# Direct products by halves of time in place of seven half-size products: gated unit and output projection

## The chip, the cores and the metric

The kernel runs on one core of a Trainium2 chip. The metric is the device time in microseconds (us) of one execution. Engines: PE is TensorE (matmul), DVE is VectorE, ACT is ScalarE, POOL is GpSimd, SP issues most DMAs.

## The reference, cut to what matters

A trunk of two layers on a stream of 1024 tokens by 1024 features. Layer 0 mixes by a long convolution beside a differential attention, joined by one output projection `w_out`; layer 1 mixes by a gated unit; each is followed by a convolutional feed-forward block (FFN).

```python
# layer 0, first mixer (y_a: convolution, y_b: attention, 512 features each)
return jnp.concatenate([y_a, y_b], axis=-1) @ w_out
# layer 1, gated unit
u, v = jnp.split(jax.nn.gelu(h @ w_in + b_in, approximate=False), 2, axis=-1)
v = layernorm(v, ln_g, ln_b)
vb = v.reshape(B, n, CHUNK, SGU_GROUPS, D_SGU // SGU_GROUPS)
s = jnp.einsum('gts,bnsgc->bntgc', w_s, vb) + b_s.T[:, :, None]
return (u * s.reshape(B, L, D_SGU)) @ w_out
# in both layers
x = x + g1 * mix_x
x = x + g2 * conv_ffn(modulate(rmsnorm(x, norm_ffn_g[i]), sh2, sc2), *ffn)
```

Four matrix products of 1024 x 1024 x 1024 are concerned: `w_out` of layer 0, the two halves (u and v) of the gated unit's `w_in`, and its `w_out`.

## The kernel before, in words

**Tiles.** The stream lies as eight tiles of 128 features x 1024 times; `H0` and `H1` are the two halves of 512 times. Every operand of a large product is split in two (`hilo`, L1149 to L1154): ACT rounds it to the upper part (the cast, L1152), DVE or POOL subtracts it from the operand for the lower part (through the helper at L128), and `mm3` issues three matmuls of 128 x 512 (L149): upper by upper, upper by lower, lower by upper. A 1024 x 1024 x 1024 product taken directly is 128 such groups, 384 matmuls.

**Seven half-size products.** Before, each such product is made of seven of half size, M1 to M7 (48 matmuls each, 336 in all). They take sums of the weight's quarters (`wsums`) and of the operand's quarters (`in_place`, or the blocks B11, B21 and T1 to T4 that `norm` writes), and each result is added to one or more quarters of the output (`gated_sum`, `accum`). `down_steps` cuts M1 to M7 into steps of one k (12 matmuls).

**The planner.** `run` goes through a list of `Step`s. Before a step's matmuls (`use`) it issues the loads of steps up to `ahead` further on, and the splits (`prep`) of steps up to `prep_ahead` further on. `Later` holds generators that put a few instructions of other work (norms, the unit's centring) between steps. The letters of tables such as `E_W` say for each split whether DVE (V) or POOL (G) subtracts. Each engine does its instructions in program order; so does each DMA queue.

**First mixer.** `heads` runs the attention. In its last heads, products M1, M2 and M6 of the output projection (`product`, 144 matmuls) fill PE between the scores, in the PSUM banks of the scores. `out_proj` does M7, M4, M5 and M3 (192 matmuls) after the attention, adds them to the stream, squares it for the row norm, and starts the FFN's norm.

**Gated unit.** `sgu` first forms u by Winograd products (`up_phase`), adds bias and Gelu and writes it to memory (`ud`); then v (`down_steps(2, ...)`), its bias, Gelu and centring by layer norm (`center`); mixing by positions in 128 x 128 matmuls; then u is read back, multiplied, and the output product follows (`down_steps(3, ...)`). Layer 0's FFN (FFN0) comes before it, layer 1's (FFN1) behind it.

```python
def hilo(x, elo=None, new=unit):
    t = new(F32R)
    A.copy(out=t[:, H0], in_=x)
    sub(elo or G, t[:, H1], x, t[:, H0])
```

Of the kernel before, what the change touches and what calls it, by code (L numbers as in the profile page):

```python
# [11 lines left out]
F32 = mybir.dt.float32  # L12
# [47 lines left out]
E_U, E_V, E_B, E_C = ("VVVV",) * 3, ("VVVV",) * 5, ("GGGGGGGG",), ("GGGGVVVV",) * 2  # L60
PO = "wtap"
# [27 lines left out]
def tile_kernel(ctx: ExitStack, tc: tile.TileContext, ap: dict, out: bass.AP, stop=None):  # L89
# [703 lines left out]
    def attention(fp, x):  # L793

        with ExitStack() as es:
# [132 lines left out]
            wb, spare, aux = {}, [], None  # L928

            def two_rows(src, k, n=2):  # L930

                r = spare.pop(0) if spare else W.pool.tile([P, 2, 512], F32, tag="wraw", name=nm("wraw"))
                ld(r[:, :n], src[k : k + n].rearrange("k p n -> p k n"))
                return r

            def parts(name, tag):
                if tag == "p":
                    t = [pp.tile([P, NKEY], F32R, tag="p", name=nm("p"), bufs=PB) for _ in range(4)]
                    hi, lo = ([t[2 * i + k // 2][:, HALF[k % 2]] for k in range(4)] for i in range(2))
                else:  # L940
                    hi, lo = ([t[:, k * 512 : (k + 1) * 512] for k in range(4)] for t in (f8(F32R), f8(F32R)))
                wb[name] = hi, lo
                return hi, lo

            def operand(name, src):

                hi, lo = parts(name, "f8")
                raw = []
                for k in (0, 2):
                    raw.append(raw_unit(src[k : k + 2].rearrange("k p n -> p k n")))  # L950
                    yield
                for k in range(4):
                    x = raw[k // 2][:, HALF[k % 2]]
                    A.copy(out=hi[k], in_=x)
                    sub(V if k == 3 else G, lo[k], x, hi[k])
                    yield

            def operand3(name, a, b, c, op, tag, last=None):

                hi, lo = parts(name, tag)  # L960
                for k in (0, 2):
                    x, y, z = two_rows(a, k, 2 if k == 0 or last is None else 1), two_rows(b, k), two_rows(c, k)
                    yield
                    for i in range(2):
                        xi = x[:, i] if k + i < 3 or last is None else last
                        yi = y[:, i]
                        op(V, yi, xi, yi)
                        (sub if op is add else add)(V, yi, yi, z[:, i])
                        A.copy(out=hi[k + i], in_=yi)
                        sub(G, lo[k + i], yi, hi[k + i])  # L970
                        yield
# [7 lines left out]
            def operands():  # L979
                yield from operand("w1", ap["wabo"][0:4][:, :, H0])  # L980
                yield from operand("w2", ap["wabo"][4:8][:, :, H0])
                yield from operand("b1", yd[0:4][:, :, H0])
                wo = ap["wabo"]
                yield from operand3("w6", wo[0:4][:, :, H1], wo[4:8][:, :, H1], wo[0:4][:, :, H0], add, "p")

            def product(m):

                (wh, wl), (bh, bl) = wb["w" + m[1]], wb["b" + m[1]]
                accum = gated_sum(x, mods[0][:, 16:24])
                ps = [scores_bank(j // 2)[:, :1024] if j % 2 == 0 else None for j in range(4)]  # L990
                ps = [ps[j // 2 * 2][:, HALF[j % 2]] for j in range(4)]
                order = [(k, j) for j in range(4) for k in range(4)] if m != "M6" else [(k, j) for k in range(4) for j in range(4)]
                for n, (k, j) in enumerate(order):
                    js = slice(j * P, (j + 1) * P)
                    mm3(ps[j], wh[k][:, js], wl[k][:, js], bh[k], bl[k], k == 0, k == 3)
                    if k == 3:
                        accum(m, j, ps[j])
                    if n % 4 == 3:
                        yield
# [4 lines left out]
            def heads():  # L1004
                nonlocal aux
                aux = f8(F32).rearrange("p (a n) -> p a n", a=4)
                V.memset(aux[:, 0, 0:1], 0.0)
# [19 lines left out]
                def nrm():  # L1027
                    if norms and next(norms[0], 1):
                        norms.pop(0)

# [54 lines left out]
                for _ in side:  # L1085
                    pass
                for _ in product("M1"):
                    pv()
                    nrm()
                for _ in operand("b2", yd[4:8][:, :, H0]):  # L1090
                    pass
                for _ in range(2):
                    r = f8(F32).rearrange("p (a k n) -> p a k n", a=2, k=2)
                    spare.extend((r[:, 0], r[:, 1]))
                b6 = operand3("b6", yd[4:8][:, :, H1], yd[0:4][:, :, H1], yd[0:4][:, :, H0], sub, "p", aux[:, 3])
                for _ in product("M2"):
                    pv()
                    nrm()
                    nrm()
                    next(b6, None)  # L1100
# [3 lines left out]
                for _ in b6:  # L1104
                    pass
                for _ in product("M6"):
                    pass
# [90 lines left out]
    class Stream:  # L1198
        T = None

# [33 lines left out]
    def norm(x, sqs, l, a, b):  # L1234
# [39 lines left out]
        for n, i in (("T1", 0), ("B22", 4)):  # L1274
            for k in range(4):

                T[n][k] = hilo(x[i + k][:, H1], E(E_5[s], i + k), unit if i + k == 0 else xunit)
                yield k % 2

# [173 lines left out]
    def residual(s, x, gate, dst, after):  # L1453
# [17 lines left out]

        def done(m):
# [8 lines left out]
    def then_norm(x, a, b):  # L1481
        return lambda l, sqs: Later.add(norm(x, sqs, l, a(), b()), N0[sqs.s][l])

# [3 lines left out]
    def out_proj(x):  # L1487
        y, ts = [None] * NK, [None] * 4
        def bload(m, k):
            if m == "M7":  # L1490
                for i in (k, k + 4):
                    y[i] = unit()
                    ld(y[i], yd[i])

        def bprep(m, k, _):
            return hilo(in_place(0, m, k, y[k], y[k + 4], ts, "M7"), E(E_O[0], k))

        acc, done, start = residual(0, x, mods[0][:, 16:24], xs[0], then_norm(x, lambda: A2[0], lambda: mods[0][:, 24:32]))
        start()
        if T3P:  # L1500
            t = unit()
            G.memset(t[:, 0:1], 0.0)
            ts[0:2] = [t[:, H0], t[:, H1]]
        steps = down_steps(0, 4, ap["wabo"], bload, bprep, acc, done, products=ORDER[3:])
        for s in steps[4:]:
            s.ahead = 16
        prep = steps[SQ].prep
        steps[SQ].prep = lambda: (prep(), done("M2"))
        return steps
# [80 lines left out]
    def sgu(x_src, dst):  # L1590
        ud = dram.tile([NK, P, S], F32, name="ud")
        v, u, t3, k_ = [None] * NK, [None] * NK, [None] * 4, {}

        def post(m, c1, c2):
            for c, g in ((c1, m), (c2, m + 4)):
                A.activation(c, c, AF.Gelu, bias=col("sbu", g))
                st(ud[g], c)
# [19 lines left out]
        def accum(m, j, p):  # L1617
            if m == "M1":
                for t in (j, j + 4):
                    v[t] = unit()  # L1620
                    A.copy(out=v[t].rearrange("p (a n) -> p a n", a=2), in_=p[:, None, :].to_broadcast([P, 2, 512]))
                return
            for i, l in {"M2": [(0, 0)], "M6": [(None, 1), (1, 0)], "M7": [(1, 0), (1, 1)], "M4": [(1, 0)],
                         "M5": [(None, 1)], "M3": [(0, 1)]}[m]:
                y = v[j + 4 * l]
                if i is None:
                    y, p_ = y.rearrange("p (a n) -> p a n", a=2), p[:, None, :].to_broadcast([P, 2, 512])
                else:
                    y, p_ = y[:, HALF[i]], p
                add(V, y, y, p_)  # L1630

        def bias():
            for t in range(NK):
                add(E(E_B[0], t), v[t], v[t], k_["bv"])
                yield 1

        def center(l):


            for t in range(4 * l, 4 * l + 4):  # L1640
                x = v[t]
                A.activation(x, x, AF.Gelu)
# [10 lines left out]
            yield MIXWAIT  # L1653
            for k in range(4):
                for g in (k, k + 4):
                    ps, t = bank(), unit()[:, H0]
                    for n in range(4):
# [153 lines left out]
```

## Time and profile before

| quantity | us |
|---|---|
| median of three runs (2870.97 to 2883.97) | 2875.83 |
| the profiled execution | 2883.27 |
| its span on the core | 2881.5 |
| output projection and first norm, 933 to 1050 | 117 |
| FFN0, 1090 to 1793 | 703 |
| gated unit, 1793 to 2122 | 329 |
| FFN1 and final norm, 2190 to the end | 691.5 |

Times within a stage are read in us from the span's start. A view by windows tells how long each engine was busy in a stretch and which clock PE was granted (1.00 is full speed). The timeline lists an engine's instructions, and in brackets the idle time ahead of them and what ended it. A matmul "b<-u,u" reads two split operands and writes a PSUM bank.

### The profile page before, as it was taken

How to read it: one execution, taken by the hardware profiler on the slowest of the kernel's cores; microseconds unless marked ns; L12 is line 12 of the kernel's file. 1: busy time of each engine (PE TensorE's matmuls, PEld its weight loads, DVE VectorE, ACT ScalarE, POOL GpSimd, SP SyncE). 2: the span in 40 equal slices, each digit the busy share in tenths (PEclk: the TensorE clock that was granted, in tenths of full speed). 3: DMA queues.
4: the chain of work that ended last, by engine and by line, in shares of the span. 5: the costliest groups of instructions: out<-in, count | busy, mean ns of one | idle time of the engine just before them, and what ended most of it. 6: DMA issues, size and time to landing. Idle time of an engine off the chain costs nothing. (4 is left out here: it accounts for less than half of the span.)

```text
span 2881.5 us, 30329 instructions
## 1 busy us (share of the span) xinstructions
PE 2496.0 (87%) x11000; PEld 1965.2 (68%) x11000; DVE 2267.2 (79%) x2425; ACT 1072.5 (37%) x1561; POOL 1610.4 (56%) x986
## 2 busy tenths in 40 slices
PE   6899668777988679999999898899769999999897
PEld 2797556565766456777777686677557777777676
DVE  4676887866998788988887967868978888886954
ACT  2322111115664244334334344532344343344242
POOL 1323665544443664655556777545765555657785
PEclk9899888888999889999999999899879999999999
DMA  7133221256741532454456533243112323227422
GB/s 269 63 135 125 73 88 44 83 181 199 212 121 63 204 110 85 162 174 154 143 168 244 174 127 99 60 163 107 49 54 68 112 75 102 93 72 274 139 84 103
DMA packets 137574, 363.97 MB, mean 126 GB/s; under 512 B 12587, under 2 KB 25391, under 8 KB 135248
## 3 DMA queue, kind: packets, MB, share of 16 engines
q1 hardware_dynamic: 90768, 259.25, 28.0%
q10 hardware_dynamic: 46656, 102.78, 9.5%
q8 instruction: 87, 1.43, 0.2%
q14 instruction: 63, 0.52, 0.1%
HBM read 271.80 MB, written 90.18 MB: 126 GB/s over the span
## 5 line engine op out<-in xcount | busy, mean ns | idle before, releaser
L149 PE MATMUL b<-u,u 128*128 128x512 f32 x5780 | 1417.3, 403 | 151.4 <-POOL u L128 96.7
L149 PEld LDWEIGHTS b<-u,u 128*128 128x128 f32 x5780 | 1106.7, 195 | 459.3 <-POOL u L128 133.1
L128 POOL TENSOR_TENSOR u<-u,u 128x512 fp32r<-128x512 f32 (+2 forms) x641 | 1030.7, 1631 | 586.8 <-ACT u L1152 456.6
L128 DVE TENSOR_TENSOR u<-u,u 128x512 fp32r<-128x512 f32 (+2 forms) x569 | 640.9, 1155 | 209.6 <-ACT u L1152 133.4
L1152 ACT CAST u<-u 128x512 fp32r<-128x512 f32 x772 | 438.1, 616 | 600.1 <-DVE u L128 419.3
L124 DVE SCALAR_TENSOR_TENSOR u<-u,cols,u 128x1023 f32<-128x1023 f32 x176 | 303.8, 1729 | 23.8 <-ACT u L1520 23.0
L128 DVE TENSOR_TENSOR u<-u,b 128x512 f32<-128x512 f32 (+1 forms) x368 | 248.4, 690 | 28.5 <-PE b L149 22.8
L149 PE MATMUL b<-x,u 128*128 128x512 f32 x1008 | 246.2, 398 | 0.0
L128 POOL TENSOR_TENSOR f<-f 128x256 f32<-128x256 f32 (+2 forms) x99 | 124.7, 1273 | 210.9 <-DVE f L128 181.4
L149 PEld LDWEIGHTS b<-x,u 128*128 128x128 f32 x1008 | 190.4, 189 | 49.3 <-issue 4.2
L128 DVE TENSOR_TENSOR f<-f 128x256 f32<-128x256 f32 (+3 forms) x178 | 178.5, 1052 | 1.1
L124 DVE SCALAR_TENSOR_TENSOR x<-b,mods,x 128x512 f32<-128x512 f32 (+1 forms) x140 | 124.7, 938 | 37.8 <-PE b L149 37.8
L149 PE MATMUL pj<-hh,whi 128*128 128x512 f32 x320 | 131.5, 411 | 24.2 <-DVE t L124 14.0
L1520 ACT ACTIVATE u<-u,cols 128x1024 f32<-128x1024 f32 x88 | 109.3, 1244 | 94.4 <-DVE u L128 93.8
L128 POOL TENSOR_TENSOR p<-p,p 128x1280 f32<-128x1280 f32 x27 | 79.4, 2942 | 99.2 <-ACT p L880 78.7
L149 PE MATMUL pj<-hh,wlo 128*128 128x512 f32 x320 | 129.8, 406 | 2.4 <-DVE wlo L128 1.6
L149 PE MATMUL pj<-hl,whi 128*128 128x512 f32 x320 | 130.6, 408 | 0.0
L1532 ACT ACTIVATE u<-u 128x1024 f32<-128x1024 f32 x44 | 46.7, 1061 | 162.3 <-DVE u L124 162.2
L128 POOL TENSOR_TENSOR wlo<-wraw,whi 128x1024 fp32r<-128x1024 f32 x24 | 63.2, 2635 | 75.5 <-ACT whi L143 64.3
L869 ACT ACTIVATE p<-s,nx 128x1280 f32<-128x1280 f32 x64 | 85.0, 1329 | 43.9 <-DVE nx L865 39.9
L149 PE MATMUL s<-f,f 128*128 128x512 f32 (+1 forms) x288 | 86.2, 432 | 17.3 <-ACT t L768 9.9
L865 DVE TENSOR_REDUCE nx<-s 128x1 f32<-128x1280 f32 x64 | 94.5, 1479 | 3.8 <-PE s L149 3.3
(222 smaller groups left out, 2936.2 us busy)
## 6 DMA issues: line engine op xcount, KB each, us to landing
u<-wup SPq DMA_DIRECT2D x88, 512.0 KB, 3.6
Td<-u ACTq DMA_DIRECT2D x66, 512.0 KB, 3.8
u<-Td SPq DMA_DIRECT2D x56, 512.0 KB, 5.0
wraw<-modw SPq DMA_DIRECT2D x48, 512.0 KB, 4.4
u<-wdown SPq DMA_DIRECT2D x40, 512.0 KB, 6.5
wraw<-modw0b SPq DMA_DIRECT2D x32, 512.0 KB, 3.9
xs<-x ACTq DMA_DIRECT2D x48, 256.0 KB, 2.5
x<-xs SPq DMA_DIRECT2D x24, 512.0 KB, 4.3
```

The source lines that it names most:

```text
L124: eng.scalar_tensor_tensor(out=o, in0=a, scalar=sc, in1=b, op0=op0, op1=op1)
L128: eng.tensor_tensor(out=o, in0=a, in1=b, op=op)
L149: T.matmul(o, l, r, start=st, stop=sp)
L865: V.reduce_max(out=q.nx, in_=q.s, axis=AX.X, negate=True)
L869: A.activation(q.p[m], q.s, AF.Exp, bias=q.nx, accum_out=q.l[:, m : m + 1])
L1152: A.copy(out=t[:, H0], in_=x)
L1520: A.activation(a, c, AF.Identity, bias=col(f"fb{l}", f), scale=col(f"fw{l}1", f))
L1532: A.activation(g, g, AF.Silu)
```

## The change

All four products are taken directly, by halves of time: `l` is the half of time, `c` the half of the output's features, `k` the 128 input features of a step.

- In the attention's last heads, `mixed` splits the eight operand tiles of the first half of time and `columns` the weights (from `wabm`, the same weight laid out by blocks of output features); `product` does the whole first half of time, eight groups of 24 matmuls, in the score banks. Operand tile 7 waits for the last head norm of that half (`norms_done`).
- `out_proj` becomes 16 steps of `direct_steps` for the second half of time. Squares of the first half start at its first split.
- The norm in front of the gated unit becomes `norm_direct`: eight splits per half, no sums.
- The gated unit forms v first, with bias and Gelu at its eviction, centres each half of time (`center`), mixes, then forms u (16 steps of 24 matmuls), multiplies it at once (`gate`) and goes on to the output product. u is no longer written to memory.
- In the instruction streams PE has 10356 matmuls instead of 10164 (48 more in the first mixer, 144 more in the gated unit); DVE has 2191 instructions instead of 2419, ACT 1655 instead of 1727, POOL 922 instead of 991.

```diff
+SV, SW, SO, SP = (8, 3), (4, 2), (8, 4), (16, 4)
+E_H, E_X, E_Y = ("VGVGVGVG", "VGVGVGVG"), "VGVG", ("VGVGVGVG", "VGVGVGVG")
+A_Y, A_W = "GGGVGGVV", "GGVGVGVG"
...
+            def product():
+
+                for m in range(NK):
+                    if m % 2 == 0:
+                        ps = scores_bank(m // 2 % 2)
+                    while m not in wb:
+                        yield True
+                    p = ps[:, HALF[m % 2]]
+                    for k in range(NK):
+                        while yb[k] is None:
+                            yield True
+                        kk = slice(k * P, (k + 1) * P)
+                        mm3(p, wb[m][0][:, kk], wb[m][1][:, kk], *yb[k], k == 0, k == NK - 1)
...
+                    y = x[m][:, H0]
+                    stt(V, y, p, gate[:, m : m + 1], y, MUL, ADD)
...
+    def norm_direct(x, sqs, l, a, b):
...
+        for k in range(NK):
+            mul(E(E_M[s], k), x[k][:, c], x[k][:, c], R)
+            A.activation(x[k][:, c], x[k][:, c], AF.Identity, bias=b[:, k : k + 1], scale=a[:, k : k + 1])
+            Stream.H[l][k] = hilo(x[k][:, c], E(E_H[l], k), xunit if l and k else unit)
...
+        def prep(l, c, k):
+            if l == ls[0]:
+                w[c, k] = hilo(raw.pop((c, k)), E(E_X, k % 4))
+            if c == 0 and bsrc is not None:
+                bs[l, k] = hilo(bs[l, k], E(E_X, (k + 1) % 4))
+
+        def use(l, c, k):
...
+            for j in range(4):
+                js = slice(j * P, (j + 1) * P)
+                if swap:
+                    mm3(ps[j], bh[:, js], bl[:, js], wh, wl, k == 0, k == NK - 1)
+                else:
+                    mm3(ps[j], wh[:, js], wl[:, js], bh, bl, k == 0, k == NK - 1)
...
     def out_proj(x):
...
-        steps = down_steps(0, 4, ap["wabo"], bload, bprep, acc, done, products=ORDER[3:])
...
+        steps = direct_steps(ap["wabo"], None, acc, done, *SP, ls=(1,), bsrc=yd)
+        prep = steps[0].prep
+        steps[0].prep = lambda: (prep(), done(0, 0), done(0, 1))
...
+        def accum(l, c, j, p):
+            t = 4 * l + j
+            if c == 0:
+                v[t] = unit()
+            add(V, v[t][:, HALF[c]], p, k_["bv"][:, HALF[c]])
+            A.activation(v[t][:, HALF[c]], v[t][:, HALF[c]], AF.Gelu)
...
+            t = mixed[g][:, HALF[l]]
+            mul(E(E_C[l], g), t, t, u)
+            y[l][g] = hilo(t, E(E_Y[l], g))
...
-        steps = up_phase([(m, ap["wsu"][m], ap["wsu"][m + 4]) for m in range(4)], post, 1)
-        vs = down_steps(2, 4, ap["wsv"], None, None, accum, done, resident=True)
...
+        steps = direct_steps(ap["wsv"], lambda l, k: Stream.H[l][k], accum, done, *SV, swap=True)
...
-        steps += down_steps(3, 4, ap["wso"], lambda m, k: None, bprep, acc, dn, (x, x_src))
+        steps += direct_steps(ap["wso"], lambda l, k: y[l][k], acc, dn, *SO, x=(x, x_src))
```

SP, where the second half's loads of the output projection begin (`yd` is the mixed stream in memory, `wabo` the weight). Before:

```order
L933 DMA wraw_5870<-yd 128x2x512 [waits Pool_49]
L933 DMA wraw_5872<-yd 128x2x512 [waits DMAHW0_49,Pool_49]
L1357 DMA u_5979<-wabo 128x2x512 [waits DMAHW4_49,DMAHW0_49,DVE_49]
L1357 DMA u_5981<-wabo 128x2x512 [waits DMAHW5_49]
L1357 DMA u_5983<-wabo 128x2x512 [waits DMAHW6_49]
```

and of the changed kernel:

```order
L181 DMA wraw_5814<-wabm 128x1024 [waits DMAHW1_49,DVE_49]
L1510 DMA u_5979<-yd 128x2x512 [waits DMAHW7_49,DVE_49,PE_49]
L1514 DMA u_5981<-wabo 128x2x512 [waits DMAHW2_49,DMAHW1_49,Pool_49]
L1510 DMA u_5983<-yd 128x2x512 [waits DMAHW2_49]
L1514 DMA u_5985<-wabo 128x2x512 [waits DMAHW3_49]
```

The first of these loads takes a tile whose memory the score product's operands hold, so that it now waits for PE too.

POOL in the same stage, around the first half's row norm (`sv` is its variance, `x_...<-x_...,u_6106` its products with the broadcast row, `u_5993` raw weights). Before:

```order
L1502 MEMSET u_5974 128x1
L128 TENSOR_TENSOR u_6000<-u_5979,u_6000 128x512
L128 TENSOR_TENSOR u_6006<-u_5974,u_6006 128x512
L128 TENSOR_TENSOR u_5974<-u_5993,u_5991 128x512
L128 TENSOR_TENSOR u_5991<-u_5991 128x512
L128 TENSOR_TENSOR u_5991<-u_5993,u_5991 128x512
```

and of the changed kernel:

```order
L1212 TENSOR_TENSOR sv_6103<-sv_6103,mhalf 128x4
L132 TENSOR_TENSOR u_6114<-u_5991,u_6114 128x512
L132 TENSOR_TENSOR x_5103<-x_5103,u_6106 128x512
L132 TENSOR_TENSOR x_5111<-x_5111,u_6106 128x512
L132 TENSOR_TENSOR x_5107<-x_5107,u_6106 128x512
L132 TENSOR_TENSOR u_6139<-x_5109,u_6139 128x512
L132 TENSOR_TENSOR u_6142<-u_5993,u_6142 128x512
```

The sums of operands and weights are gone; the last row, the lower part of the weight of step k = 7, now stands behind three products of the norm.

PE in the gated unit, where the second half of time is mixed (128x128, `u_123..` are centred tiles of v). Before:

```order
L149 MATMUL b_13328<-u_13246,u_13243 128x512
L149 MATMUL b_13343<-u_12505,u_12656 128x128
L149 MATMUL b_13351<-u_12505,u_12656 128x128
L149 MATMUL b_13379<-u_12505,u_12656 128x128
L149 MATMUL b_13387<-u_12505,u_12656 128x128
L149 MATMUL b_13328<-u_13246,u_13243 128x512 x2
```

and of the changed kernel:

```order
L153 MATMUL b_12373<-u_12128,x_11990 128x512 x3
L153 MATMUL b_12545<-u_11722,u_12351 128x128
L153 MATMUL b_12551<-u_11722,u_12351 128x128
L153 MATMUL b_12565<-u_11481,u_12471 128x512 x3
L153 MATMUL b_12565<-u_11504,u_12471 128x512 x3
L153 MATMUL b_12545<-u_11722,u_12354 128x128
```

The mixing moved from the middle of the output product to a place directly behind the last product of v.

## Rows read from the trace of the kernel before

**Rows 1.** The page's busy time: us, share of the span, instructions.

```profile
PE 2496.0 (87%) x11000; PEld 1965.2 (68%) x11000; DVE 2267.2 (79%) x2425; ACT 1072.5 (37%) x1561; POOL 1610.4 (56%) x986
```

**Rows 2.** Windows: length, busy of PE, PEld, DVE, ACT, POOL; PE's clock; DMA.

```profile
1090.00:1793.00 703.00, 680.90 (x3029) 529.77 (x3029) 581.35 (x574) 292.59 (x444) 430.23 (x267) 0.98 0.46 155
1793.00:2122.00 329.00, 280.24 (x1164) 218.72 (x1162) 267.64 (x327) 128.28 (x203) 189.65 (x126) 0.91 0.28 95
2190.00:2881.50 691.50, 628.60 (x2614) 495.27 (x2612) 526.93 (x501) 262.68 (x391) 441.02 (x289) 0.97 0.34 115
...
966.40:1049.50 83.10, 56.40 (x210) 41.73 (x210) 72.28 (x79) 32.39 (x57) 66.45 (x37) 0.79 0.39 138
```

**Rows 3.** Timeline of PE, output projection: start, length, count, idle before and releaser.

```profile
941.81 1.10 PE L149 MATMUL tr<-f,ones 128*128 128x512 f32 x2 [0.39 <-DVE f L242]
...
965.41 0.96 PE L149 MATMUL s<-p,p 128*128 128x512 f32 x3 [0.88 <-DVE x L124]
973.37 0.79 PE L149 MATMUL b<-u,u 128*128 128x512 f32 x1 [7.00 <-ACT u L1152]
983.33 5.09 PE L149 MATMUL b<-u,u 128*128 128x512 f32 x12 [9.17 <-POOL u L128]
...
994.03 18.44 PE L149 MATMUL b<-u,u 128*128 128x512 f32 x71 [1.81 <-POOL u L128]
```

**Rows 4.** Timeline of PE in the gated unit.

```profile
1797.23 1.05 PE L149 MATMUL b<-ones,u 128*128 128x1 f32 x8 [1.26 <-DVE u L128]
...
1818.12 4.64 PE L149 MATMUL b<-u,u 128*128 128x512 f32 x10 [2.31 <-POOL u L128]
...
1890.06 22.88 PE L149 MATMUL b<-u,u 128*128 128x512 f32 x99
...
1974.00 1.95 PE L149 MATMUL b<-u,u 128*128 128x128 f32 x16
...
2034.42 0.80 PE L149 MATMUL b<-u,u 128*128 128x512 f32 x1 [5.00 <-ACT u L1152]
...
2130.77 1.87 PE L149 MATMUL b<-ones,u 128*128 128x1 f32 x8 [5.45 <-DVE u L128]
```

**Rows 5.** Timeline of DVE: a head norm, last evictions of three stages, the centring.

```profile
933.04 0.73 DVE L124 SCALAR_TENSOR_TENSOR f<-f,sg,tr 128x512 f32<-128x512 f32 x1
...
1047.54 2.79 DVE L124 SCALAR_TENSOR_TENSOR x<-b,mods,x 128x512 f32<-128x512 f32 x4
...
1791.25 2.79 DVE L124 SCALAR_TENSOR_TENSOR x<-b,mods,x 128x512 f32<-128x512 f32 x4 [4.38 <-PE b L149]
...
1987.80 0.68 DVE L1645 BATCH_NORM_STATS2 st<-u 128x6 f32<-128x512 f32 x1
...
1998.05 0.81 DVE L1651 TENSOR_SCALAR u<-u,mv,rs 128x1024 f32<-128x1024 f32 x1 [0.66 <-POOL rs L1650]
...
2119.77 2.73 DVE L124 SCALAR_TENSOR_TENSOR x<-b,mods,x 128x512 f32<-128x512 f32 x4 [1.96 <-PE b L149]
```

**Rows 6.** Groups of the gated unit, 1793 to 2122: count, busy us, mean ns.

```profile
L128 POOL TENSOR_TENSOR u<-u,u 128x512 fp32r<-128x512 f32 x69 | 105.3, 1545 | 53.4 <-ACT u L1152 48.3 <-DVE u L128 5.0
L1152 ACT CAST u<-u 128x512 fp32r<-128x512 f32 x115 | 64.8, 617 | 121.0 <-DVE u L128 81.2 <-POOL u L128 27.1 <-PE b L149 7.4
...
L128 DVE TENSOR_TENSOR u<-u,u 128x512 fp32r<-128x512 f32 x44 | 53.6, 1232 | 20.0 <-ACT u L1152 20.0
L128 DVE TENSOR_TENSOR u<-u,b 128x512 f32<-128x512 f32 x52 | 33.8, 677 | 14.6 <-PE b L149 12.6 <-DMA u<-wsv 2.0
```

**Rows 7.** Timeline of POOL: one subtraction with DVE quiet beside it.

```profile
941.96 1.28 POOL L128 TENSOR_TENSOR f<-wraw,f 128x512 fp32r<-128x512 f32 x1 [1.41 <-ACT f L954]
```

**Rows 8.** SP's queue: start, time that four issues took.

```profile
953.07 1.91 SPq L1357 DMA_DIRECT2D u<-wabo  x4
```

**Rows 9.** DMA issues: count, KB each, median us from issue to landing.

```profile
u<-yd SPq DMA_DIRECT2D x8, 512.0 KB, 8.7
...
f<-yd SPq DMA_DIRECT2D x3, 512.0 KB, 3.6
```

More of the change, by code (lines that the diff above doesn't have):

```diff
@@ L951, in operand @@
                     yield
[L952 to L955, printed above, removed]
-                    yield
[L958 to L962, printed above, removed]
-                    yield
[L964 to L971, printed above, removed]
+                for k, r in enumerate(raw + [aux[:, 2]] * (4 - len(raw))):
+                    while k0 + k == 7 and norms_done[0] < 7:
+                        yield
+                    A.copy(out=hi[k], in_=r)
+                    sub(E(A_Y, k0 + k), lo[k], r, hi[k])
+                    yb[k0 + k] = hi[k], lo[k]
+                    yield
@@ L979, in operands @@
             def operands():
[L980 to L999, printed above, removed]
+                yield from mixed(0)
+                for m in range(2):
+                    yield from columns(m)
+                yield from mixed(4)
+            def product():
[10 more added lines that the diff above has]
+                        mm3(p, wb[m][0][:, kk], wb[m][1][:, kk], *yb[k], k == 0, k == NK - 1)
+                        if k == 3:
+                            yield
+                    y = x[m][:, H0]
+                    stt(V, y, p, gate[:, m : m + 1], y, MUL, ADD)
+                    yield
             class Obj:
@@ L1499, in out_proj @@
[L1499 to L1503, printed above, removed]
-        steps = down_steps(0, 4, ap["wabo"], bload, bprep, acc, done, products=ORDER[3:])
[L1505 to L1508, printed above, removed]
+        acc, done, _ = residual(0, x, mods[0][:, 16:24], xs[0],
+                                then_norm(x, lambda: A2[0], lambda: mods[0][:, 24:32]), True)
@@ L1590, in sgu @@
     def sgu(x_src, dst):
[L1591 to L1597, printed above, removed]
+        v, mixed, y, k_ = [None] * NK, [None] * NK, [[None] * NK, [None] * NK], {}
         def consts():
@@ new lines, in sgu, with done, gate, uload @@
+        mixed_n = [0, 0]
+        def done(l, c):
+            if (l, c) == (0, 0):
+                Later.add(offsets())
+            if c:
+                Later.add(center(l))
+        def gate(g, l, u):
+            while mixed_n[l] <= g:
+                yield 1
+            t = mixed[g][:, HALF[l]]
+            mul(E(E_C[l], g), t, t, u)
+            y[l][g] = hilo(t, E(E_Y[l], g))
+        w = {}
+        def uload(m):
+            w[m] = unit()
+            ld(w[m], ap["wsu"][m])
+        def uprep(m):
+            w[m] = [hilo(w[m][:, c], E(E_W[1], (2 * m + i) % 7)) for i, c in enumerate(HALF)]
@@ new lines, in uuse @@
+        def uuse(m, l):
+            ps = bank()
+            for k in range(NK):
+                kk, (wh, wl) = slice(k % 4 * P, (k % 4 + 1) * P), w[m][k // 4]
+                mm3(ps, wh[:, kk], wl[:, kk], *Stream.H[l][k], k == 0, k == NK - 1)
+            if l == 0:
+                w["u"] = unit()
+            u = w["u"][:, HALF[l]]
+            A.activation(u, ps, AF.Gelu, bias=col("sbu", m))
+            Later.add(gate(m, l, u))
+        steps = direct_steps(ap["wsv"], lambda l, k: Stream.H[l][k], accum, done, *SV, swap=True)
```

188 lines of the change are left out of this document (90 added, 98 removed).

## The prediction

> **What bounds the kernel now.** I read the page's busy time first, then the stages by windows, then PE's timeline inside the two stages that the change touches. PE is busy 87% of the span, DVE 79% and POOL 56% [rows 1], so the mean points at PE, and a change that adds matmuls would seem to lose. The stages say otherwise [rows 2]: in FFN0 PE is busy 680.90 of 703 us at a clock of 0.98, while in the gated unit it is busy 280.24 of 329 us at 0.91, and in the output projection's second part only 56.40 of 83.1 us at 0.79. There PE is not the limit. Its idle time ends on a cast or on a POOL subtraction: 7.00 and 9.17 us at the start of the output projection [rows 3], 5.00 us in the gated unit's last product [rows 4]. What is late are operands: sums on DVE and POOL, then a cast, then the subtraction. The direct product pays with matmuls where PE has room and takes away the sums that PE waits for. The question is whether the idle time is larger than the matmuls added, and whether the splits that remain keep up.
>
> **The price of a matmul.** 99 matmuls in 22.88 us without a gap [rows 4]: 0.2311 us each, 2.77 us for a step of 12. The 192 added ones are 44.4 us by that row: 11.1 in the first mixer and 33.3 in the gated unit. The Trainium skill ("TensorE: Matmul & The Clock Gate", section "Wait — 56ns, not 53.3ns?") gives 215.7 ns for a 512-column matmul on a warm array; by it alone the 192 would be 41.4 us, 3 less than by the row, and the row decides here.
>
> **First mixer.** I follow PE from the last head norm of the first half of time, which DVE starts at 933.04 and does in 0.73 us [rows 5]. Operand tile 7 is its output: a cast of 0.62 [rows 6] and a DVE subtraction of about 0.7 (between 0.677 of a DVE addition [rows 6] and the norm's own 0.73), with some 0.2 for the hand-overs, an estimate: ready at 935.3. In program order 161 of the score product's 192 matmuls stand behind this split: 37.2 us. Other work of the last heads is two small groups of about 1.1 us [rows 3], and group m = 7 waits some 1.1 us for the eviction of m = 6, whose bank pair it shares (one eviction is 0.7 us, 2.79 for four [rows 5]). The product ends at 975.7.
>
> Then comes a wait that was not there. The loads of the second half go into memory that the product's operands hold till its last matmul; before, they were issued at 953 while M6 was still running [rows 8]. So PE stands still for two issues of 0.48 us [rows 8], a landing, two casts (1.24) and a POOL subtraction of 1.28 [rows 7]. The landing is 3.6 us for the quiet load of this kind and 8.7 for the one in a crowd [rows 9]; I take 4.5, near the lower, since the first of the crowd is wanted and not the middle one, and keep both ends (minus 1, plus 4) for the range. The second half's matmuls start at 975.7 + 0.9 + 4.5 + 2.5 = 983.6.
>
> From there 192 matmuls are 44.4 us. After the idle time the first 12 run at half clock, as the 5.09 us show that 12 took at 983.33 [rows 3]: 2.3 more. The first half's row norm puts two small groups of about 1.1 between them (2.2). One wait I expect in the middle: on POOL the lower part of the weight of k = 7 stands behind three products with the norm's broadcast row; three POOL products at 1.55 [rows 6] are 4.6, so 5 us, with 0 to 10 as ends (0 if the norm is ready early, 10 if it waits for its chain as well). The first of the four last evictions can go when 9 matmuls are still to come, 2.1 us ahead of the end: 983.6 + 44.4 + 2.3 + 2.2 + 5 - 2.1 = 1035.4. Before, it stands at 1047.54 [rows 5]. **The first mixer saves 12.1 us**, 0 to 18 with the ends above. Nothing is counted for the deleted sums themselves: what they cost is the idle time that goes. Their DMAs go too; in the attention's last heads eight loads of `wabm` stand in place of those of `wabo`, issued while PE has scores to do, and I count them at nothing (if they came late, PE would wait one landing, 3.6 to 8.7).
>
> **Gated unit.** From FFN0's last evictions to the unit's own is 1791.25 to 2119.77, 328.5 us [rows 5]. After: 1152 matmuls are 266.2 us; the mixing is 128 small matmuls, 16 in 1.95 us [rows 4], so 15.6; bias offsets and row norms are six groups of 1.05 [rows 4], 6.3. Together 288.1 us, if PE never waits. The waits, each by a row: the first products of v need the normed, cast and subtracted operand of each half: 2.3 each as at 1818.12 [rows 4], 4.6. The second half's mixing now stands directly behind the last product of v. The centring of four tiles took 1987.80 to 1998.86, 11.1 us [rows 5]; ahead of it are an addition of 0.68 and Gelu, for which I take the cast's 0.62 [rows 6]; the first of the four starts 2.1 us before the product ends, and 12 matmuls of u with 8 small ones (3.8 us) stand between the waiting ones: 11.1 + 1.3 - 2.1 - 3.8 = 6.5, with 0 and 11 as ends. Behind that wait in PE's order is all of u, so nothing covers it. The last product's start waits for the final gate and its split: 3, between 2.31 and 5.00 [rows 4]. Half clock after these waits: 2.5, as in the 12 matmuls above. That is 16.6 of waits and 304.7 in all. **The gated unit saves 23.8 us.** The removed spill and reload of u, the sums and the separate bias additions lie on this path only through the waits that they caused; the loads of `wsu` and `wso` come out at nothing, since they are released at least 96 matmuls (22 us) ahead of use and land in less than 8.7 [rows 9].
>
> **Into FFN1.** From the unit's last evictions to the column sums it is 11.0 us before (2119.77 [rows 5] to 2130.77 [rows 4]), and 6.0 in the same place ahead of the gated unit (1791.25 to 1797.23), where no subtractions share DVE. After the change nothing stands between the last evictions and the sums of squares on DVE; **I take 3 of the 5**, since POOL still has its own squares to add.
>
> **The sum** is 12.1 + 23.8 + 3 = 38.9 us: 2883.27 becomes 2844.4. The profiled execution is 7.4 us (0.26%) above the median of the runs; its span is 1.8 below its own time. Off the median, 2875.83 - 38.9 = 2837.
>
> **The rivals.**
>
> Splits bind. DVE's and POOL's subtractions lengthen each other: 1232 and 1545 ns as means in the gated unit [rows 6], against about 0.7 [rows 5] and 1.28 [rows 7] by themselves. If that sets the pace, PE is busy only as much as in FFN1, 628.60 of 691.5 [rows 2], 0.909: the gated unit takes 288.1 / 0.909 = 316.9 and saves 11.6; and the second half of the output projection goes as slowly as before, 983.33 to 1047.54 or 64.2 us, from 983.6 to 1047.8, so that nothing is saved there. Then 2864, no change by measure. Against it: FFN0 keeps PE at 0.97 with the same two engines splitting, and each step now has one or two splits and no sums. The Trainium skill ("SBUF — State Buffer", section "Who interferes with whom") says that DVE, reading two operands from SBUF, and GpSimd share a port pair under an exclusive lock; by that rule the splits take turns, and the lengthened means agree with it in direction.
>
> The change doesn't do what it says in the first mixer: the second half's start stays as slow as before, 27.6 us from the last score product (966.4) to the steady run at 994.03 [rows 3], in place of the 7.9 I count, since eight loads at once land late and the first steps each want two splits. Then 19.7 of the gain go: 2857.
>
> Slower: the weight steps are too short for their splits. 48 steps (16 each of the output projection, of v and of the last product) want a new piece of weight, many with a new operand too. In the 64.2 us from 983.33 to 1047.54 before, some 32 splits were made, 2.0 us each. If each of the 48 steps waits for two at that pace, 4.0 us against 2.77, 59.5 us are added, 20.6 more than the gain: 2896. It decides from 3.58 us a step on (no gain) and 3.88 (measurably slower). Against it: half the splits of before waited for sums ahead of them, which are gone, and the groups' own busy time gives 1.2 and 1.5 us on two engines side by side.
>
> **How the numbers follow.** I give the forecast 0.67, the slow start 0.10, binding splits 0.15, the too short steps 0.08. A measurement of this kernel can tell about 0.5% from no change, 14.4 us: faster is below 2861.5, slower above 2890. The forecast and the slow start are faster (0.77), binding splits are the same (0.15), the short steps slower (0.08). The forecast's own range is 2820 to 2852. If all waits that I priced were gone (5 + 2.3 + 16.6 = 24 us), the time would be 2813; the upper end takes in binding splits: 2813 to 2866.
>
> **What would show it.** In the profile after: PE's clock and busy share in the gated unit up to some 0.95; the longest gap at the start of the second half of the output projection, 7 to 9 us, ended by a DMA or the split behind it; a wait of about 5 us at step k = 7 ended by POOL; one of about 6.5 us between v and u ended by DVE L1651's centring; the last evictions of the first mixer near 1035 and a gated unit of about 305 us. The prediction is wrong if gaps of 1 us or more stand ahead of most weight steps, or if the matmuls run at half clock outside the starts.

## The result, and the profile after

The changed kernel takes 2811.65 us (median of four runs, 2809.20 to 2813.79) against 2877.59 of the kernel before in the same rounds: 65.9 us less, a ratio of 0.9766 with a 95% interval of 0.975 to 0.9783. The direction was forecast, the size was not: 38.9 us were forecast, and 2811.65 lies below the range's lower end of 2813. The two profiled executions, 2883.27 and 2809.20, lie 74.1 us apart.

The page's busy time after, to be held against [rows 1]:

```profile
PE 2490.2 (89%) x11192; PEld 1971.8 (70%) x11192; DVE 2051.5 (73%) x2197; ACT 1028.5 (37%) x1497; POOL 1475.3 (53%) x917
```

PE has 192 matmuls more and is busy 5.8 us less, because less of its work runs at half clock, where twelve took 5.09 us at 983.33 [rows 3] against 2.77 by the long row of [rows 4]. DVE lost 216 us, POOL 135. The two stages by windows (length, busy of PE, PEld, DVE, ACT, POOL, PE's clock, DMA), the output projection's second half and the gated unit between the column sums ahead of it and those behind it:

```profile
966.40:1034.50 68.10, 53.98 (x211) 41.23 (x212) 50.48 (x46) 30.98 (x55) 44.18 (x28) 0.87 0.54 191
1766.90:2059.30 292.40, 284.69 (x1299) 233.40 (x1298) 118.36 (x172) 89.33 (x148) 100.49 (x76) 0.99 0.21 69
```

Before, the unit between the same two marks:

```profile
1797.20:2130.80 333.60, 279.87 (x1161) 218.44 (x1161) 272.31 (x329) 128.79 (x204) 194.36 (x128) 0.91 0.28 93
```

In the unit PE's busy share rises from 0.84 to 0.97 and its clock from 0.91 to 0.99, while DVE's share falls from 0.82 to 0.40. PE's idle time falls from 53.7 to 7.7 us, and the 144 added matmuls, 33.3 us by [rows 4], cost only 4.8 us of busy time, as the clock rose. PE's timeline after, in the first mixer (the score product's end, the start of the second half, the column sums of the first half, then those of FFN0):

```profile
960.64 5.69 PE L153 MATMUL s<-f,f 128*128 128x512 f32 x24 [0.94 <-DVE x L128]
972.99 0.80 PE L153 MATMUL b<-u,u 128*128 128x512 f32 x1 [6.66 <-ACT u L1140]
974.34 8.68 PE L153 MATMUL b<-u,u 128*128 128x512 f32 x29 [0.55 <-POOL u L132]
989.37 1.87 PE L153 MATMUL b<-ones,u 128*128 128x1 f32 x8 [6.35 <-DVE u L132]
...
1038.32 1.05 PE L153 MATMUL b<-ones,u 128*128 128x1 f32 x8
```

and in the gated unit, where the five idle times shown are all of its 7.7 us:

```profile
1766.94 0.95 PE L153 MATMUL b<-ones,u 128*128 128x1 f32 x8
...
1770.14 1.12 PE L153 MATMUL b<-u,ones 128*128 128x512 f32 x2 [0.75 <-DVE u L1215]
...
1791.77 0.96 PE L153 MATMUL b<-u,u 128*128 128x512 f32 x3 [1.48 <-DVE u L132]
...
1868.20 11.61 PE L153 MATMUL b<-u,u 128*128 128x128 f32 x59 [3.63 <-DVE mv L1670]
...
1884.56 9.90 PE L153 MATMUL b<-u,u 128*128 128x128 f32 x59
...
1965.42 47.99 PE L153 MATMUL b<-u,u 128*128 128x512 f32 x211
...
2016.45 1.13 PE L153 MATMUL b<-u,ones 128*128 128x512 f32 x2 [0.75 <-DVE u L1215]
...
2059.29 1.05 PE L153 MATMUL b<-ones,u 128*128 128x1 f32 x8 [1.11 <-DVE u L132]
```

DVE's timeline: the last head norm of the first half of time, the split of operand tile 7, splits and additions of squares ahead of the first half's column sums, the mixer's last evictions, evictions of v, and the unit's last evictions, with what comes behind the last evictions:

```profile
923.08 0.75 DVE L128 SCALAR_TENSOR_TENSOR f<-f,sg,tr 128x512 f32<-128x512 f32 x1 [1.28 <-PE tr L153]
924.88 0.69 DVE L132 TENSOR_TENSOR f<-f,f 128x512 fp32r<-128x512 f32 x1 [1.05 <-ACT f L949]
...
982.01 5.11 DVE L132 TENSOR_TENSOR u<-u,u 128x512 fp32r<-128x512 f32 x3
987.05 2.27 DVE L132 TENSOR_TENSOR u<-u,sq 128x512 f32<-128x512 f32 x3
...
1032.48 2.79 DVE L128 SCALAR_TENSOR_TENSOR x<-b,mods,x 128x512 f32<-128x512 f32 x4 [2.79 <-PE b L153]
1035.19 3.07 DVE L132 TENSOR_TENSOR u<-u,sq 128x512 f32<-128x512 f32 x4
...
1791.03 2.48 DVE L132 TENSOR_TENSOR u<-b,u 128x512 f32<-128x512 f32 x4
...
2053.46 2.79 DVE L128 SCALAR_TENSOR_TENSOR x<-b,mods,x 128x512 f32<-128x512 f32 x4 [8.82 <-PE b L153]
2056.16 3.07 DVE L132 TENSOR_TENSOR u<-u,sq 128x512 f32<-128x512 f32 x4
```

The column sums of before on PE's timeline (the first half's in the mixer, FFN0's, the gated unit's first ones), and the unit's first ones after:

```profile
1026.54 1.87 PE L149 MATMUL b<-ones,u 128*128 128x1 f32 x8 [6.72 <-DVE u L128]
...
1059.18 1.60 PE L149 MATMUL b<-ones,u 128*128 128x1 f32 x8 [2.37 <-DVE u L128]
...
1737.77 0.95 PE L149 MATMUL b<-ones,u 128*128 128x1 f32 x8
```

```profile
1708.79 0.95 PE L153 MATMUL b<-ones,u 128*128 128x1 f32 x8
```

Where the 74 us went, mark by mark (starts on the timelines of the two profiles):

| stretch | before | after | saved | forecast |
|---|---|---|---|---|
| start to the score product's end | 966.4 | 966.3 | 0.0 | inside the mixer |
| to the mixer's last evictions | 81.2 | 66.2 | 15.0 | 12.1 |
| to FFN0's column sums | 11.6 | 5.8 | 5.8 | none |
| FFN0, to the unit's first column sums | 678.6 | 670.5 | 8.1 | none |
| to the unit's second column sums | 59.5 | 58.2 | 1.3 | none |
| unit, to its last evictions | 322.5 | 286.5 | 36.0 | 23.8 |
| to FFN1's column sums | 11.0 | 5.8 | 5.2 | 3 |
| FFN1 and final norm | 750.7 | 748.1 | 2.6 | none |

Without FFN0's 8.1 the rows sum to 65.9, as the medians have it; that they agree so closely is luck. The table rests on one pair of profiles, and its first row is not steady: the score product ends between 961 and 970 us in three profiles with the first mixer of before (this one, the one taken again and the one with the new unit alone), and between 966 and 976 in eleven with the new one, some 5 us later on the mean.

### The profile page after: what moved, and what is told of

Same layout as the page of the kernel before. It is cut to its first block, busy times and chain, and to the rows that moved or that the text cites. A ratio compares the mean times of both kernels' runs of the same rounds, so it can differ in the third digit from the quotient of the medians.

```text
span 2807.4 us, 30194 instructions
## 1 busy us (share of the span) xinstructions
PE 2490.2 (89%) x11192; PEld 1971.8 (70%) x11192; DVE 2051.5 (73%) x2197; ACT 1028.5 (37%) x1497; POOL 1475.3 (53%) x917
## 5 line engine op out<-in xcount | busy, mean ns | idle before, releaser
L153 PE MATMUL b<-u,u 128*128 128x512 f32 x5756 | 1372.8, 396 | 95.0 <-POOL u L132 66.2
L153 PEld LDWEIGHTS b<-u,u 128*128 128x128 f32 x5756 | 1081.0, 191 | 383.6 <-POOL u L132 97.9
L132 POOL TENSOR_TENSOR u<-u,u 128x512 fp32r<-128x512 f32 (+1 forms) x582 | 910.9, 1585 | 612.4 <-ACT u L1140 498.7
L132 DVE TENSOR_TENSOR u<-u,u 128x512 f32<-128x512 f32 (+2 forms) x476 | 537.7, 1151 | 263.3 <-ACT u L1140 161.2
L1140 ACT CAST u<-u 128x512 fp32r<-128x512 f32 x712 | 405.2, 616 | 491.2 <-DVE u L132 325.8
L128 DVE SCALAR_TENSOR_TENSOR u<-u,cols,u 128x1023 f32<-128x1023 f32 x176 | 303.7, 1729 | 23.8 <-ACT u L1564 23.0
L153 PE MATMUL b<-x,u 128*128 128x512 f32 x1092 | 267.0, 398 | 0.0
L153 PEld LDWEIGHTS b<-x,u 128*128 128x128 f32 x1092 | 206.2, 189 | 53.4 <-issue 3.4
L132 DVE TENSOR_TENSOR u<-u,b 128x512 f32<-128x512 f32 x308 | 205.7, 679 | 13.9 <-PE b L153 10.1
L128 DVE SCALAR_TENSOR_TENSOR x<-b,mods,x 128x512 f32<-128x512 f32 (+1 forms) x104 | 88.8, 906 | 69.9 <-PE b L153 69.9
L153 PE MATMUL s<-f,f 128*128 128x512 f32 (+1 forms) x288 | 80.4, 412 | 16.9 <-ACT t L772 9.9
```

Source lines behind the costliest of these rows:

```text
L128: eng.scalar_tensor_tensor(out=o, in0=a, scalar=sc, in1=b, op0=op0, op1=op1)
L132: eng.tensor_tensor(out=o, in0=a, in1=b, op=op)
L153: T.matmul(o, l, r, start=st, stop=sp)
```

## The experiments

Each ratio is against the kernel before in the same rounds, on the same chip; the kernel before had medians of 2881 to 2884 us there.

**The kernel before once more.**

> The kernel before, unchanged, profiled once more. Its first profile took 678.6 us from FFN0's own column sums (1059.18) to the gated unit's first ones (1737.77), the changed kernel 670.5 us for the same 2106 + 462 products. If the 8.1 us are chance between executions, this profile shows 670 to 674 there and a span of 2870 to 2876. If the change gives them (by the clock or by what runs at FFN0's start), it shows 677 to 680 again.

Measured: 2887.67 us. FFN0 took 678.6 us again:

```profile
1062.98 1.60 PE L149 MATMUL b<-ones,u 128*128 128x1 f32 x8 [2.38 <-DVE u L128]
...
1741.61 0.95 PE L149 MATMUL b<-ones,u 128*128 128x1 f32 x8
```

The mixer, the ways to the column sums and FFN0 repeat to 0.1 us; the part up to the score product's end is 3.8 us longer, the unit 1.0 longer and FFN1 0.4 shorter. Chance as the whole cause of FFN0's 8.1 is not borne out by this run.

**Each half of the change alone.** The first kernel has the direct first mixer with the gated unit and norm of before; the second the reverse.

> Only the first mixer is changed (score product and output projection direct); the gated unit and its norm are those of before. Theory A (the stages are worth what the two profiles show, each by itself): 15.1 us up to the last evictions of the mixer and 5.8 from there to FFN0's column sums, 20.9 in all, so 2855 to 2860. Theory B (FFN0's 9.4 us belong to the mixer's change as well): 30, so 2845 to 2850. Rival C (the mixer pays only together with the unit): 2870 or more.

> Only the gated unit and the norm ahead of it are changed; attention and output projection are those of before. Theory A: 35.9 us in the unit and 5.2 from its last evictions to FFN1's column sums, 41, so 2834 to 2840. If FFN0's 9.4 us belong to the unit's change (its loads and splits begin in FFN0's tail): 50, so 2825 to 2830. By the prediction's own terms (23.8 + 3): 2849 to 2853.

Measured: 2859.19 (ratio 0.9919, 0.9902 to 0.9937) and 2835.38 (0.9844, 0.9824 to 0.9865) where the kernel before has 2882.70. By the ratios that is 23.3 and 45.0 us (18 to 28 and 39 to 51 by the intervals), together 68.3 where the whole change gives 67.5 (0.9766): the halves add. Both medians lie in theory A's ranges, and what the stages show (20.9 and 41) lies within the intervals. Theory B's 30 us for the mixer and the prediction's 26.8 for the unit with its end are out; the 50 that the unit would give with all of FFN0's gain lies just inside the interval. In both kernels FFN0 is short, 668.9 and 671.1 us, so it belongs to neither half in particular. Rival C is out.

**The changed kernel once more.**

> The changed kernel once more, for two questions. Its FFN0 (column sums to the gated unit's first ones) took 670.5 us in the first profile, those of the kernel before 678.6 in both of theirs, and kernels with the same FFN0 took 668.9 to 676.5. If that is chance between executions, this profile may lie anywhere from 668 to 679; if it belongs to the program, it is 670.5 again within 0.5. And the gain itself: 0.975 to 0.978 of the kernel before.

Measured: 2817.24 us (0.9773, 0.9752 to 0.9793), so the gain repeats. FFN0 took 673.2 us: the same program gives 670.5 and 673.2, so part of its spread is chance. Over all kernels with one FFN0 code it lies between 668.9 and 678.6.

**The row norm later.**

```diff
-N0 = ((1, 1), (6, 1), (1, 1), (1, 0))
+N0 = ((4, 1), (6, 1), (1, 1), (1, 0))
```

> The changed kernel with the first half's row norm in the output projection put three steps (36 matmuls, 8.3 us) later; one number changed. PE waits 6.35 us ahead of the column sums at 989.37, for additions of squares on DVE that stand behind three splits. Theory: the wait is one of order, and moving the sums back fills it with matmuls: 4 to 6 us faster than the changed kernel, 2806 to 2808. Rival: DVE and POOL have no room there, and the wait only moves behind the sums or to FFN0's start: 2810 to 2814.

Measured: 2814.89 us, 0.9774 (0.9752 to 0.9796), no gain. PE's timeline shows the wait gone and its price elsewhere:

```profile
981.59 15.63 PE L153 MATMUL b<-u,u 128*128 128x512 f32 x59 [0.56 <-POOL u L132]
999.08 1.59 PE L153 MATMUL b<-ones,u 128*128 128x1 f32 x8 [1.87 <-DVE u L132]
1000.53 5.47 PE L153 MATMUL b<-u,u 128*128 128x512 f32 x12
...
1046.86 1.58 PE L153 MATMUL b<-ones,u 128*128 128x1 f32 x8 [1.79 <-DVE u L132]
1048.30 5.47 PE L153 MATMUL b<-u,u 128*128 128x512 f32 x12
```

The 6.35 us became 1.87, but from the second half's first matmul to FFN0's column sums it is 66.6 us (980.23 to 1046.86) against 65.3 (972.99 to 1038.32). Behind the last evictions DVE now has three other sums between its additions of squares, so that the column sums come 7.5 us after them in place of 5.8, and PE waits there again (1.79 us). The 12 matmuls behind that wait run at a clock of 0.50 and take 5.47 us, where the changed kernel has 3.01 at 1.00; behind the first half's column sums both kernels run at 0.50. The rival held.

**The sums' load put back, on and off the chain.** Three DVE operations on each of the unit's 48 weight pieces, in place, or into a tile that nobody reads:

```diff
+    def extra(r, aside=False):
+        o = unit()[:, H0] if aside else r
+        for _ in range(3):
+            V.tensor_tensor(out=o, in0=r, in1=r, op=ALU.max)
...
```

> The changed kernel; each of the gated unit's 48 weight pieces (128x512) gets three two-operand DVE operations in place ahead of its split (the maximum of the piece with itself: values unchanged), 144 in all, so that DVE has about the load back that the sums were: 144 at 0.68 to 1.2 us are 98 to 173 us on top of 132. Theory A (the waits of before came from DVE's and POOL's load in this stage): PE waits again, the unit becomes 20 to 45 us longer, here and with the operations aside. Theory B (from the chain: a split that must wait for its sums): 20 us or more here, next to nothing with the operations aside. Rival C (neither: the splits lie three and four steps ahead and hide both; the waits of before came from the seven products' own order): under 8 us here and aside.

> The same 144 DVE operations, but written to a tile that nobody reads, so that no split waits for their results. Theory A (load): as much longer as with the operations in place, 20 to 45 us. Theory B (chain): under 8 us, against 20 or more in place. Rival C: under 8 us in both.

Measured: 2830.67 (0.9821, 0.9800 to 0.9841) and 2835.02 (0.9829, 0.9807 to 0.9851). The unit, by the same marks as above:

```profile
1771.50:2078.10 306.60, 292.22 (x1289) 237.64 (x1289) 221.22 (x300) 91.28 (x148) 129.37 (x76) 0.96 0.19 66
```

```profile
1779.60:2085.90 306.30, 289.37 (x1286) 235.25 (x1286) 223.78 (x304) 89.77 (x148) 122.06 (x76) 0.97 0.20 66
```

The first row is with the operations in place, the second with them aside: 306.6 and 306.3 us against 292.4, and some 4 us in the norm ahead. That both cost the same rules out the chain (B); 14 us is more than C and less than the 20 that load (A) was to give at least. The operations aside also take a tile of the pool each time, those in place none, so the tiles are not what costs here.

**The splits put back, and both.** Each weight piece is split once more into a tile that nobody reads; then this together with the operations aside.

```diff
+                if unit_only:
+                    hilo(raw[c, k], E(E_X, (k + 1) % 4))
                 w[c, k] = hilo(raw.pop((c, k)), E(E_X, k % 4))
...
+            for i, c in enumerate(HALF):
+                hilo(w[m][:, c], E(E_X, i))
```

> The changed kernel; each of the gated unit's 48 weight pieces is split once more into a tile that nobody reads (a cast on ACT, a subtraction on DVE or POOL in turns): 48 of the some 50 splits that the seven products had more. Theory A (load): with the splits back PE waits again, 10 to 30 us in the unit. Rival C (the splits lie ahead and POOL has room): under 5 us.

> Both loads at once: the 48 idle splits and the 144 idle DVE operations, which alone gave 14 us in the unit and 4 in the norm ahead of it. Theory A (load is all of it): DVE and POOL are then as busy as before the change, and the unit, 292.4 us from the second half's column sums to FFN1's, becomes 340 to 360, since PE also has the added matmuls. Rival (part of the waits of before came from the order of the seven products): 310 to 330.

Measured: 2820.81 (0.979, 0.9762 to 0.9818) and 2864.99 (0.993, 0.9906 to 0.9955). The unit with the splits, and with both:

```profile
1773.40:2072.70 299.30, 286.97 (x1297) 233.77 (x1295) 160.05 (x194) 111.48 (x191) 136.70 (x98) 0.99 0.20 67
```

```profile
1780.00:2113.40 333.40, 299.43 (x1275) 239.97 (x1275) 265.47 (x326) 112.17 (x191) 159.61 (x98) 0.93 0.18 62
```

The splits alone add 6.9 us, the sums 13.9, both 41.0. With both, DVE is busy 265 us, near the 272 of before, though POOL has only 160 of its 194, and the unit takes 333.4 us against 333.6 before, though the order is that of the changed kernel. It is not the same time over again. Of the 41.0 us, 26.3 are idle time of PE (7.7 to 34.0, where before had 53.7) and 14.7 its longer busy time, at a clock of 0.93. PE's matmuls of split operands now wait for DVE most, where before they waited for casts and for POOL, as the groups (count, busy us, mean ns, idle time before them) show, first before, then with both loads:

```profile
L149 PE MATMUL b<-u,u 128*128 128x512 f32 x840 | 221.3, 423 | 39.7 <-ACT u L1152 18.1 <-POOL u L128 14.8 <-DVE u L128 4.4
```

```profile
L153 PE MATMUL b<-u,u 128*128 128x512 f32 x787 | 203.7, 418 | 27.4 <-DVE u L132 19.2 <-ACT u L1140 5.6 <-POOL u L132 2.6
```

So load is enough to take the whole gain of the unit away. The 333.4 us lie between the two ranges, nearer to the rival's 330 than to the 340 of load alone. That load was the whole cause before is therefore not shown: the order of the seven products is not told apart from it, since the kernel of before has 144 matmuls fewer here, and the idle splits also hold tiles that other work could use.

**The mixing later.**

```diff
+            if l == 1:
+                yield 2
             for g in range(NK):
```

> The changed kernel with the second half's mixing put two steps of u (48 matmuls, 11 us) later; one line. PE waits 3.63 us at 1868.20 for the centring ahead of the mixing. Theory (a wait of order, with room elsewhere): the unit gets 3 to 4 us shorter, 2808 on the chip that gave 2811.65. Rival: the gates that need the mixing come late in turn and the last product waits: no change or up to 5 us longer.

Measured: 2806.63 us, 0.9732 (0.9712 to 0.9751). The wait of 3.63 us is gone, and the mixing runs in one piece of 9.90 us in place of 11.61 behind the wait:

```profile
1771.20:2058.10 286.90, 282.85 (x1299) 232.22 (x1297) 119.40 (x172) 89.34 (x148) 100.47 (x76) 1.00 0.21 70
```

```profile
1868.65 6.32 PE L153 MATMUL b<-u,u 128*128 128x512 f32 x27
...
1879.72 9.90 PE L153 MATMUL b<-u,u 128*128 128x128 f32 x59
```

The unit is 5.5 us shorter, more than the 3 to 4 expected: the 3.63 of the wait, and 1.7 because the mixing behind it no longer starts at half clock (in the changed kernel PE's clock is 0.59 in the first 2.3 us behind the wait). The rival is out.

**The first load's tile elsewhere.** The head norm's tile `aux` is allocated behind the first head's loads.

```diff
+                kqv = [load_head(0)]
                 aux = f8(F32).rearrange("p (a n) -> p a n", a=4)
...
-                tiles, kqv, vals, norms = [], [load_head(0)], [], []
+                tiles, vals, norms = [], [], []
```

> The changed kernel; the head norm's tile is allocated behind the first head's loads, so that it, and not a tile of the score product's operands, lies where the first load of the output projection's second half goes. The load then waits for the last head norm's store and no more for the product's last matmul. Theory (the 6.66 us gap at 966.33 is that load's wait, its landing and the splits): the gap falls to about 1 us, 5 to 6 us off the mixer, from 66.2 us (last score product to last evictions) to 60 or 61. Rival (the wait that follows, 6.35 us for the additions of squares, grows by as much, since those start at the first split too): under 2 us.

Measured: 2810.47 us, 0.9753 (0.9729 to 0.9777). The loads go out from 956.62, ahead of the product's end, and the gaps of 6.66 and 0.55 become three of 4.8 in sum; the wait for the squares stays:

```profile
956.62 0.38 SPq L1511 DMA_DIRECT2D u<-yd  x1
```

```profile
978.37 0.50 PE L153 MATMUL b<-u,u 128*128 128x512 f32 x1 [2.38 <-ACT u L1141]
979.72 5.73 PE L153 MATMUL b<-u,u 128*128 128x512 f32 x24 [0.85 <-POOL u L132]
986.98 1.43 PE L153 MATMUL b<-u,u 128*128 128x512 f32 x5 [1.53 <-POOL u L132]
994.75 1.86 PE L153 MATMUL b<-ones,u 128*128 128x1 f32 x8 [6.34 <-DVE u L132]
```

From the product's end (975.99) to FFN0's column sums it is 67.9 us against 72.0: 4.1 us in the trace. That is less than the 5 to 6 expected, since the gap did not fall to 1 us, and more than the rival's 2. The ratio cannot tell this from the changed kernel.

**Both edits.**

> The changed kernel with both edits that gained: the mixing two steps later (the unit went from 246.3 to 240.8 us between its column sums) and the head norm's tile elsewhere (4.1 us between the last score product and FFN0's column sums). If they add, 9.6 us off the changed kernel in the same rounds, 2800 to 2804 on a chip where that has 2811; rival: the waits that are left take up part of it, 5 us or less.

Measured: 2807.11 us against 2817.24 of the changed kernel in the same rounds, 0.9743 (0.9722 to 0.9763) of the kernel before. By the marks the two edits add: the unit takes 286.9 us against 293.2, and from the product's end to FFN0's column sums it is 68.0 us against 71.7, 10.0 in sum. The medians of the same rounds agree: 10.1 us less, where 9.6 were expected. Against the later mixing alone the ratios show no gain (0.9743 and 0.9732); only the marks in the trace do.

```profile
1771.00:2057.90 286.90, 282.79 (x1298) 232.18 (x1296) 119.45 (x172) 89.52 (x148) 100.48 (x76) 1.00 0.21 70
```

## Why the prediction was wrong in size

**The reading of the bound was right.** PE waited for operands, and the direct product took the waits away: PE is busy 0.97 of the unit after. The rivals fell: binding splits would have left the unit at 317 us, the slow start did not come (the first row of the second half starts 6.66 us after the product, where 7.9 was counted), and weight steps that are too short showed nowhere.

**The step that failed: the price of the gated unit after the change.** Pure matmuls were counted as 288.1 us, waits and half clock as 16.6, together 304.7. The same stretch took 292.7, which is 12.0 less. The waits were counted as 14.1; PE's rows up to the last evictions have 6.6 of idle time. The waits at the starts of v (4.6) and of the last product (3) did not come, and the mixing's 6.5 came to 3.63. Not counted had been two waits of 0.75 for a row norm and one of 1.48 that, by its time, ends on v's first eviction (`u<-b,u`, from 1791.03 on). The half clock was counted as 2.5; the 59 matmuls behind the mixing's wait take 11.61 us where as many at 1884.56 take 9.90, so that it came to 1.7. The pure matmuls took the rest, 284.4, which is 3.7 less than counted. The prices of the waits came from rows of before [rows 3 to 6], most of them from a stage in which DVE was busy 82% of the time; in the changed stage it is busy 40%, and none of PE's waits there ends on a split. The idle loads show this by going the other way: with both put back, PE's idle time is 34.0 us. The error was to forecast that the cause goes and to price what is left as though it stayed.

**The forgotten stretch: into FFN0.** The prediction gave 3 us to the way from the unit's last evictions to FFN1's column sums, and nothing to the same place behind the first mixer, where before the column sums came 11.6 us after the last evictions and now come 5.8 us after. Both places gained more, 5.8 and 5.2: before, nine operations stood on DVE between the unit's last evictions and the column sums, four additions of squares (`u<-u,sq`) and five other sums, some of them at 1.76 us (three of the nine, from DVE's timeline before):

```profile
2122.42 0.83 DVE L128 TENSOR_TENSOR u<-u,sq 128x512 f32<-128x512 f32 x1
2123.17 1.78 DVE L128 TENSOR_TENSOR u<-u,u 128x512 f32<-128x512 f32 x1
2124.88 1.76 DVE L128 TENSOR_TENSOR u<-u,sq 128x512 f32<-128x512 f32 x1
```

Now only the four additions of squares are left, in 3.07 us. That is 8 us more than forecast. FFN1's own 2.6 and the 1.3 us ahead of the unit were not forecast either; with the unit's 12.2 and the first mixer's 2.9 this makes the 27 us by which 65.9 exceeds 38.9.

**The first mixer: by luck a nearly right sum from wrong terms.** 15.0 against 12.1. Operand tile 7 was ready at 925.6 and not at 935.3, since the head norm stands at 923.08, ten us earlier than in [rows 5]: the time was taken from the trace of before, though in the changed order 21 matmuls of the product stand in front of that norm, where the trace of before has 36. At 0.23 us each that is some 3.5 of the ten; the rest was not followed up. The product's end moved with it, 966.3 for the forecast 975.7. The gap behind it is 1.2 us less than forecast (6.4 to 8.1 us in nine profiles of kernels with this start). Against that, the wait of 5 us at POOL's split of k = 7 did not come, and another, which had not been counted, is there: 6.35 us for the additions of squares, behind three splits on DVE. It could have been read before: the same column sums wait 6.72 us for DVE at 1026.54 there. With it, and with matmuls at half clock around it (a clock of 0.50 in the 4.7 us behind it), the second half took 59.5 us to the last evictions where 51.8 had been counted.

**The range.** Its lower end took all priced waits to be zero, but not that a stretch had been left out; with the 5.8 us into FFN0 it would have held 2811.65.

**What stays open.** FFN0 took 678.6 us in both profiles of the kernel before, 676.5 with the later norm and 668.9 to 673.7 in all the others; one program alone gave 670.5 and 673.2. Part of it stands at its start, where 12 matmuls behind the column sums take 5.47 us before and 3.01 after; the rest is not explained, and neither is why the part up to the score product's end varies by some 10 us. The two may offset each other in the medians.

## What to carry to other kernels

Where a cheaper algorithm needs sums of its operands, look at the stage's own busy shares: PE, which was idle 16% of the gated unit and below full clock in it, took 14% more large matmuls (1152 in place of 1008) in less time, because that freed the engines that feed it. When a change takes load off the feeding engines, price the waits that remain from a stage with the load that will be there, not from the one that goes. And follow the end of every changed stage to the next stage's first use: what stands on DVE behind the last evictions is part of the change.

## What the runs showed of the hardware

Added work on DVE makes POOL's own subtractions slower. POOL's splits of 128x512 (count, busy us, mean ns) in the unit of the changed kernel, with 144 operations on DVE in place, with them aside, and with the idle splits besides:

```profile
L132 POOL TENSOR_TENSOR u<-u,u 128x512 fp32r<-128x512 f32 x37 | 51.3, 1402 | 77.0 <-ACT u L1140 70.7 <-issue 5.0 <-PE b L153 1.2
```

```profile
L132 POOL TENSOR_TENSOR u<-u,u 128x512 fp32r<-128x512 f32 x37 | 76.5, 2086 | 86.7 <-ACT u L1140 74.5 <-issue 7.4 <-DVE u L132 4.8
```

```profile
L132 POOL TENSOR_TENSOR u<-u,u 128x512 fp32r<-128x512 f32 x37 | 69.6, 1897 | 64.5 <-ACT u L1140 59.6 <-PE b L153 4.9
```

```profile
L132 POOL TENSOR_TENSOR u<-u,u 128x512 fp32r<-128x512 f32 x59 | 107.8, 1847 | 79.4 <-ACT u L1140 75.6 <-DMA x<-xs 1.9 <-issue 1.5
```

37 equal instructions take 1402 ns in the first and 2086 in the second, 1.5 times as long. The Trainium skill ("SBUF — State Buffer", section "Who interferes with whom") says that GpSimd shares its SBUF ports with DVE's second pair, one holding them at a time; the trace agrees in direction and puts this price on it. It does not explain why the two loads cost 41.0 us together and 20.8 apart: POOL's mean is 1897 ns with the operations aside and no longer, 1847, with the splits besides. What the runs show is that DVE is then busy 0.80 of the unit, near its 0.82 before, and that most of PE's idle time ends on DVE; why the sum is so much more than its parts stays open.
